# First FFN of a decoder trunk on Trainium2: its input normalized ahead of the products, and a new start for the sum of squares

## Chip, cores and metric

The kernel runs on one core of one Trainium2 chip. The metric is the device time of one execution in microseconds; lower is better. Engines: TensorE (PE: matmuls; PEld: its weight loads), VectorE (DVE), ScalarE (ACT), GpSimd (POOL) and SyncE (SP, which issues the DMA loads).

## The reference

A decoder trunk of two layers on x of 256 tokens by 1024 features, all in float32. Each layer is an FFN half step, a token mixer (retention in layer 0, a short gated convolution in layer 1) and a second FFN half step. Ahead of each of these six sublayers the input is normalized and modulated:

```
def rmsnorm(x, g):
    xf = x.astype(jnp.float32)
    xf = xf * lax.rsqrt(jnp.mean(xf * xf, axis=-1, keepdims=True) + EPS)
    return xf.astype(x.dtype) * g

def modulate(x, g, shift, scale):
    return rmsnorm(x, g) * (1 + scale[:, None, :]) + shift[:, None, :]

def swiglu(h, w_in, w_out):
    gu = h @ w_in
    gate, up = gu[..., :D_FF], gu[..., D_FF:]
    return (jax.nn.silu(gate) * up) @ w_out
```

`shift`, `scale` and `gate` of every sublayer are rows of `silu(c) @ ada_w + ada_b`. A sublayer ends in `x = x + gate * y` (half of it for an FFN). D_FF is 2816, that is 22 tiles of 128. A last rmsnorm gives the output.

## The kernel before

Activations are held transposed: 128 features on the partitions, 256 tokens along the free dimension, so x is eight blocks k of 128x256. To multiply float32 with float32r matmuls, each operand is held as a high half (`hi`, a rounding cast on ScalarE, `split_high`, L248) and the rest (`lo`, a subtraction on VectorE or GpSimd, `split_low`, L253). A product of one 128x128 weight block with one block of h is hi times h's high half, hi times h's low half, and lo times h's high half (`product`, L278). If both halves of h lie side by side in one 512-column tile, the first two are one matmul of 512 columns (L288) whose two half sums are added afterwards; otherwise there are three matmuls of 256 columns (L290 to L292).

Weights stream from memory once, in 1 MB tiles of 128x2048 (`load`, L229), five buffers deep, all issued by SyncE. The weights of the modulation (`ada_w`) come the same way; VectorE multiplies a tile with `cond` (silu of c) and sums it per row in two reductions (`ada_reduce`, L116, its operation at L120). Both kinds of load share the queue.

The first sublayer is an FFN and has a start of its own. `first_modulated` (L464) loads x in four loads, squares it on VectorE and GpSimd, adds the squares in pairs, sums them over the partitions by matmuls with a matrix of ones (`total`, L361: plain f32, two records in the trace for each), and takes the root `std` on ScalarE. `fill` (L428) then issues eight small matmuls whose result nobody reads. For each k it reduces the two `ada_w` halves of that block (shift and scale), scales x by `scale` on ScalarE (L493), adds `std * shift` on VectorE (`halves`, L422, operation at L425), splits the result into halves h, and splits three of four 512-column parts of the weight tile. ScalarE, VectorE and GpSimd run this part in the written order (`manual_schedule`); elsewhere a scheduler orders instructions by priority and dependence.

x is not divided by its root here. h is `x*scale + std*shift`, and since the division is the same for all features of a token, the products are multiplied by r = 1/std afterwards, in `normalized` (L325, operation at L328), one VectorE pass over both halves (gate and up) of a tile as it leaves PSUM.

`first_projections` (L560) multiplies the first eight FFN tiles together, k outermost: in each k block 12 of 16 weight blocks as three matmuls (L579 to L581) and the last four as one plain f32 matmul (L576), into four PSUM tiles. Tiles 8 to 21 follow one at a time through `projections` (L294) with `product`; h's halves lie in a tile 264 wide, so three matmuls are issued. For every tile ScalarE applies silu (L321), VectorE multiplies with the other half (`av`, L592, three buffers), and the result `act` is split (ScalarE cast L334, GpSimd subtraction L335). There are four PSUM tiles of two banks in rotation; after eleven tiles one of them holds `cond` for good (L612).

The later FFNs already work on an h that is normalized whole: `whole` (L434) multiplies x by r (L440), applies scale and shift in one ScalarE `Identity` (L441), and stores both halves side by side in a 512-column slot; `projected` (L307) then issues the 512-column form and adds the half sums with a ScalarE copy (L315) and a VectorE add (L316). Slots come from a pool of 30 shared by `xs`, `whole`, `act` and others.

## Time and profile before

| what | value |
|---|---|
| median of 3 runs | 1078.89 us (1077.05 to 1079.44) |
| the profiled execution's own time | 1079.4 us |
| its span, first to last instruction | 1077.6 us |
| TensorE busy | 1051.5 us (98%), 6642 matmul records |
| VectorE busy | 845.5 us (78%) |
| ScalarE busy | 622.0 us (58%) |
| GpSimd busy | 410.7 us (38%) |
| memory read | 266.20 MB |

Rows of a timeline give the start, the duration, the engine, the line of the kernel, the operation, the tile written and the tiles read, shapes, how many instructions were merged, and in square brackets how long the engine stood idle before and what released it. A matmul's printed duration reaches to its last result, so consecutive matmuls overlap; their pace is read from their starts.

### The profile page before, as it was taken

What the parts mean: (1) busy time and instruction counts of PE and PEld (TensorE: products, weight loads), DVE (VectorE), ACT (ScalarE), POOL (GpSimd) and SP (SyncE); (2) the same over time, 40 slices, a digit from 0 to 9 for tenths busy, and PEclk for the clock granted to TensorE, in tenths of its full rate; (3) what the DMA queues carried; (4) which work ended last, traced back from release to release, by engine and by line L of the source; (5) the groups of instructions that cost most, each with busy time, mean ns of one, the idle gap of its engine ahead of it and who ended that gap; (6) DMA issues with size and microseconds to landing.
All of it is one profiled execution on the core that took longest, in us unless ns stands there. A gap on an engine that the chain in (4) does not pass through costs nothing.

```text
span 1077.6 us, 17508 instructions
## 1 busy us (share of the span) xinstructions
PE 1051.5 (98%) x6642; PEld 945.9 (88%) x6642; DVE 845.5 (78%) x1137; ACT 622.0 (58%) x1048; POOL 410.7 (38%) x357
## 2 busy tenths in 40 slices
PE   8999999999998999999999999999999989999996
PEld 6999988999886889888888988888898889888885
DVE  6899777899658898997777899777799888655444
ACT  4365545763366667566555766655576577655442
POOL 1034356254335432433345243335433433324352
PEclk9999999999999999999999999999999999999999
DMA  9977788868565576787679778777877544554441
GB/s 340 368 277 275 296 279 314 314 224 326 225 234 196 195 290 221 289 325 280 241 234 323 262 294 319 272 253 265 311 254 261 207 161 175 199 201 139 148 134 40
DMA packets 44566, 268.39 MB, mean 249 GB/s; under 512 B 4801, under 2 KB 6977, under 8 KB 19906
## 3 DMA queue, kind: packets, MB, share of 16 engines
q1 hardware_dynamic: 43138, 266.56, 68.1%
q8 instruction: 52, 0.85, 0.3%
q10 hardware_dynamic: 1344, 0.71, 0.2%
q14 instruction: 32, 0.26, 0.1%
HBM read 266.20 MB, written 1.05 MB: 248 GB/s over the span
## 4 chain that ended last, share of the span: by engine, by line
PE 57%; DVE 3%; issue 1%; ACT 0%; DVEq 0%; ACTq 0%
PE ps L288 33%; PE ps L292 19%; PE ps L291 2%; PE ps L290 2%; DVE lo L253 1%; DVE whole L335 0%; DVE rsum L518 0%; PE ps L361 0%; DVE h L415 0%; DVE raw L816 0%; ACT hi L248 0%; DVE xr L440 0%; DVE r L812 0%; DVE sum L328 0%; DVE av L594 0%
## 5 line engine op out<-in xcount | busy, mean ns | idle before, releaser
L253 DVE TENSOR_TENSOR lo<-raw,hi 128x1024 fp32r<-128x1024 f32 (+1 forms) x300 | 370.4, 1244 | 148.9 <-ACT hi L248 138.1
L248 ACT CAST hi<-raw 128x1024 fp32r<-128x1024 f32 (+2 forms) x408 | 377.0, 937 | 167.0 <-PE ps L288 65.5
L288 PE MATMUL ps<-whole,hi 128*128 128x512 f32 x1136 | 398.8, 396 | 2.4 <-ACT std L373 1.6
L292 PE MATMUL ps<-whole,lo 128*128 128x256 f32 x1264 | 353.8, 280 | 0.0
L253 POOL TENSOR_TENSOR lo<-raw,hi 128x384 fp32r<-128x384 f32 (+1 forms) x108 | 202.6, 1877 | 230.0 <-ACT hi L248 228.4
L288 PEld LDWEIGHTS ps<-whole,hi 128*128 128x128 f32 x1136 | 213.7, 188 | 53.3 <-ACT std L373 2.0
L292 PEld LDWEIGHTS ps<-whole,lo 128*128 128x128 f32 x1264 | 239.4, 189 | 0.1
L288 PE MATMUL ps<-act,hi 128*128 128x512 f32 x616 | 217.7, 398 | 0.6 <-DVE rsum L518 0.6
L292 PE MATMUL ps<-act,lo 128*128 128x256 f32 x704 | 197.8, 281 | 0.0
L335 POOL TENSOR_TENSOR act<-av,act 128x256 fp32r<-128x256 f32 x88 | 81.9, 933 | 202.4 <-ACT act L334 201.6
L120 DVE CUSTOM_DVE_ANT_0 raw<-raw,ps,misc 128x1024 f32<-128x1024 f32 x124 | 154.7, 1274 | 0.0
L288 PEld LDWEIGHTS ps<-act,hi 128*128 128x128 f32 x616 | 115.7, 188 | 29.7 <-DVE rsum L518 1.6
L292 PEld LDWEIGHTS ps<-act,lo 128*128 128x128 f32 x704 | 133.1, 189 | 0.3 <-DVE lo L253 0.3
L290 PE MATMUL ps<-h,hi 128*128 128x258 f32 (+1 forms) x464 | 131.8, 284 | 1.0 <-DVE sum L328 0.9
L291 PE MATMUL ps<-h,hi 128*128 128x258 f32 (+1 forms) x464 | 131.0, 282 | 1.5 <-DVE h L415 1.4
L292 PE MATMUL ps<-h,lo 128*128 128x258 f32 (+1 forms) x464 | 130.3, 281 | 0.0
L291 PEld LDWEIGHTS ps<-h,hi 128*128 128x128 f32 x464 | 87.9, 190 | 2.5 <-DVE h L415 2.4
L290 PEld LDWEIGHTS ps<-h,hi 128*128 128x128 f32 x464 | 87.6, 189 | 1.5 <-ACT sg L321 1.1
L292 PEld LDWEIGHTS ps<-h,lo 128*128 128x128 f32 x464 | 87.6, 189 | 0.0
L334 ACT CAST act<-av 128x256 fp32r<-128x256 f32 x88 | 35.3, 405 | 77.0 <-DVE av L592 70.5
L316 DVE TENSOR_TENSOR sum<-ps,sum 128x512 f32<-128x512 f32 x71 | 48.7, 685 | 19.7 <-ACT sum L315 19.7
L321 ACT ACTIVATE sg<-sum 128x256 f32<-128x256 f32 x79 | 32.6, 415 | 47.7 <-DVE sum L316 25.7
(135 smaller groups left out, 1425.4 us busy)
## 6 DMA issues: line engine op xcount, KB each, us to landing
raw<-in_ffn_in SPq DMA_DIRECT2D x80, 1024.0 KB, 4.9
raw<-in_ada_w SPq DMA_DIRECT2D x64, 1024.0 KB, 5.1
raw<-in_ffn_out SPq DMA_DIRECT2D x64, 704.0 KB, 5.1
raw<-in_ada_w SPq DMA_DIRECT2D x16, 512.0 KB, 7.2
raw<-in_ffn_in SPq DMA_DIRECT2D x16, 512.0 KB, 8.2
raw<-in_ret_g SPq DMA_DIRECT2D x8, 1024.0 KB, 4.9
raw<-in_ret_qk SPq DMA_DIRECT2D x8, 1024.0 KB, 5.3
raw<-in_ret_v SPq DMA_DIRECT2D x8, 1024.0 KB, 5.0
```

Of the source, the lines that this page charges most:

```text
L120: ins = nc.vector.tensor_tensor_reduce(out=w, in0=w, in1=state["cond"], scale=1.0, scalar=misc[:, C_ADAB + 72 * l + col:C_ADAB + 72 * l + ...
L248: nc.scalar.copy(out=hi, in_=raw[:, c:c + m])
L253: eng.tensor_tensor(out=lo, in0=raw, in1=hi, op=ALU.subtract)
L288: nc.tensor.matmul(out=ps, lhsT=hi, rhs=m.rearrange("p n s -> p (n s)"), start=start, stop=False)
L290: nc.tensor.matmul(out=ps, lhsT=hi, rhs=m[:, 0], start=start, stop=False)
L291: nc.tensor.matmul(out=ps, lhsT=hi, rhs=m[:, 1], start=False, stop=False)
L292: nc.tensor.matmul(out=ps[:, :n], lhsT=lo, rhs=m[:, 0], start=False, stop=stop)
L316: nc.vector.tensor_tensor(out=y[:, :, :S], in0=ps[:, :, :S], in1=y[:, :, :S], op=ALU.add)
L321: nc.scalar.activation(out=out, in_=y[:, i, :S], func=AF.Silu)
L334: hi = nc.scalar.copy(out=dst[:, 0], in_=src)
L335: lo = eng.tensor_tensor(out=dst[:, 1], in0=src, in1=dst[:, 0].bitcast(F32), op=ALU.subtract)
```

## The change

h of the first FFN is normalized before the products. The reciprocal of `std` is taken at once, after the reductions of block 0; VectorE divides x of block k+1 (`divided`) while block k is split; ScalarE applies scale and shift in one `Identity`, and the halves lie side by side in a slot `whole` of 512 columns. `normalized` is no longer called in this FFN: the first eight tiles go from PSUM to `activate` as they are, and tiles 8 to 21 go through `projected` with its 512-column matmuls, its copy and its add. x comes in two loads of four blocks instead of four of two. The squares of the first half are VectorE's, those of the second half ScalarE's (after `cond`); they are not added in pairs, and `total` takes all eight. GpSimd has no part in the sum, and the Sqrt table is loaded after the squares. The low half of block 0's h is made ahead of its first weight `lo`, that of the others behind it. Instructions that were issued behind the last two of `first_modulated` (one on ScalarE, one on VectorE) are now issued behind one on VectorE.

```
--- before.py
+++ after.py
@@ -98,8 +98,8 @@
             out=ps[:, i, :], lhsT=ones[:1, :], rhs=cond[:1, i * 512:(i + 1) * 512], start=True, stop=True
         )
     conditioned = nc.scalar.activation(out=cond, in_=ps.rearrange("p n c -> p (n c)"), func=AF.Silu)
-    x_pairs = [const.tile([P, 2, S], F32, name=f"x{i}") for i in range(KB // 2)]
-    x = [x_pairs[k // 2][:, k % 2, :] for k in range(KB)]
+    x_quads = [const.tile([P, 4, S], F32, name=f"x{i}") for i in range(KB // 4)]
+    x = [x_quads[k // 4][:, k % 4, :] for k in range(KB)]
 
 
     mod = [const.tile([P, 72], F32, name=f"mod{l}") for l in range(DEPTH)]
@@ -369,8 +369,11 @@
             ps = banks()[:, 0, :S]
         total(parts, ps, start)
         with tc.high_priority(PRIO):
-            std = tmp.tile([P, S], F32, name="std")
-            nc.scalar.activation(out=std, in_=ps, func=AF.Sqrt, bias=eps, scale=1.0 / n_feat)
+            return root(ps, n_feat)
+
+    def root(ps, n_feat):
+        std = tmp.tile([P, S], F32, name="std")
+        nc.scalar.activation(out=std, in_=ps, func=AF.Sqrt, bias=eps, scale=1.0 / n_feat)
         return std
 
     def inverse(std):
@@ -418,12 +421,6 @@
             )
             norm.setdefault("h", []).append(h[:, :, :S1])
             norm["made"] = [hi.ins, lo.ins]
-
-    def halves(l, s, k, xs, std, h):
-
-        shift = mod[l][:, 24 * s + k:24 * s + k + 1]
-        nc.vector.scalar_tensor_tensor(out=xs, in0=std, scalar=shift, in1=xs, op0=ALU.mult, op1=ALU.add)
-        return (h,) + split(h, xs, nc.vector)
 
     def fill(n):
 
@@ -467,45 +464,64 @@
         parts = []
         engines = {mybir.EngineType.Activation, mybir.EngineType.DVE, mybir.EngineType.Pool}
         with tc.manual_schedule(engines=engines):
-            for i, pair in enumerate(x_pairs):
-                nc.sync.dma_start(out=pair, in_=a["x"][:, 2 * i:2 * i + 2, :])
+            for i, quad in enumerate(x_quads):
+                nc.sync.dma_start(out=quad, in_=a["x"][:, 4 * i:4 * i + 4, :])
             nc.scalar.dma_start(out=misc, in_=a["misc"])
             ada = [ada_load(l, s, 0, 2)]
-            with tc.issue_after(conditioned.ins):
-                load_table(AF.Sqrt, ones)
             ps = banks()[:, 0, :S]
-            for i in range(2):
-                sqs = []
-                for j, eng in ((2 * i, nc.vector), (2 * i + 1, nc.gpsimd)):
-                    sq = tmp.tile([P, 2, S], F32, name=f"sq{j}", tag="rot" if i else "sum")
-                    eng.tensor_tensor(out=sq, in0=x_pairs[j], in1=x_pairs[j], op=ALU.mult)
-                    sqs.append(sq)
-                (nc.gpsimd if i else nc.vector).tensor_tensor(out=sqs[0], in0=sqs[0], in1=sqs[1], op=ALU.add)
-                total([sqs[0][:, 0, :], sqs[0][:, 1, :]], ps, i == 0, i == 1)
-            std = tmp.tile([P, S], F32, name="std")
-            nc.scalar.activation(out=std, in_=ps, func=AF.Sqrt, bias=eps, scale=1.0 / D)
+            for i, quad in enumerate(x_quads):
+                for j in range(2):
+                    sq = tmp.tile([P, 2, S], F32, name=f"sq{i}", tag="rot" if i else "sum")
+                    pair = quad[:, 2 * j:2 * j + 2, :]
+                    if i == 0:
+                        nc.vector.tensor_tensor(out=sq, in0=pair, in1=pair, op=ALU.mult)
+                    else:
+                        with tc.issue_after(conditioned.ins):
+                            nc.scalar.activation(out=sq, in_=pair, func=AF.Square)
+                    total([sq[:, 0, :], sq[:, 1, :]], ps, i == 0 and j == 0, i == 1 and j == 1)
+            load_table(AF.Sqrt, ones)
+            std = root(ps, D)
             fill(FILL)
+            ada_reduce(l, s, 0, ada.pop(), True)
+            r = inverse(std)
+
+            def divided(k):
+                if k % 2 == 0:
+                    pairs.append(in_halves(slot(F32, "xs")))
+                xs = pairs[-1][:, k % 2, :]
+                nc.vector.tensor_tensor(out=xs, in0=x[k], in1=r[:, :S], op=ALU.mult)
+                return xs
+
+            pairs = []
+            xs = divided(0)
             for k in range(KB):
-                ada_reduce(l, s, k, ada.pop(), True)
-                if k % 2 == 0:
-                    pair = in_halves(slot(F32, "xs"))
-                xs = pair[:, k % 2, :]
-                nc.scalar.activation(out=xs, in_=x[k], func=AF.Copy, scale=scale_t[l][s][:, k:k + 1])
+                if k:
+                    ada_reduce(l, s, k, ada.pop(), True)
                 raw, width, w = load(2)
                 if k + 1 < KB:
                     ada.append(ada_load(l, s, k + 1, 2))
                 first = split_high(raw, width, w, 512)
-                h = xhl_p.tile([P, 2, HALF], F32R, name=f"h{k}")[:, :, :S]
-                parts.append(halves(l, s, k, xs, std, h))
+                nc.scalar.activation(
+                    out=xs, in_=xs, func=AF.Identity, scale=scale_t[l][s][:, k:k + 1],
+                    bias=mod[l][:, 24 * s + k:24 * s + k + 1],
+                )
+                h = in_halves(slot(F32R, "whole"))
+                nc.scalar.copy(out=h[:, 0], in_=xs)
                 plain.append((xs, raw))
-                split_low(*first, nc.vector)
+                after = divided(k + 1) if k + 1 < KB else None
+                if k:
+                    split_low(*first, nc.vector)
+                made = nc.vector.tensor_tensor(out=h[:, 1], in0=xs, in1=h[:, 0].bitcast(F32), op=ALU.subtract)
+                parts.append(h)
+                if not k:
+                    split_low(*first, nc.vector)
                 for c in range(1, WHOLE // 512):
                     split_low(*split_high(raw, width, w, 512), nc.vector)
                 if k == 1:
                     load_table(AF.Silu, std)
-            r = inverse(std)
-        state["after"] = [i.ins for i in parts[-1][1:]]
-        return [p[0] for p in parts], r
+                xs = after
+        state["after"] = [made.ins]
+        return parts
 
     def residual(n, d, ps):
         l, s = sublayers[n]
@@ -581,7 +597,7 @@
                     nc.tensor.matmul(out=out, lhsT=lo, rhs=h[k][:, 0], start=False, stop=stop)
         return [ps.rearrange("p (n s) -> p n s", s=S) for ps in pss]
 
-    def ffn(n, src=None, h=None, r=None):
+    def ffn(n, src):
         act = []
 
         def activate(y, bias):
@@ -599,15 +615,12 @@
             act.append(t)
 
         if n == 0:
-            for ps in first_projections(h):
-                activate(normalized(ps, r, S), None)
+            for ps in first_projections(src["whole"]):
+                activate(ps, None)
         else:
             src["whole"] = whole(n, src["r"])
         while len(act) < FB:
-            if n:
-                activate(*projected(src))
-            else:
-                activate(normalized(projections(h), r, S), None)
+            activate(*projected(src))
             if n == 0 and len(act) == KEEP:
                 kept = banks().rearrange("p n c -> p (n c)")
                 nc.scalar.copy(out=kept, in_=cond)
@@ -794,7 +807,7 @@
 
     for n, (l, s) in enumerate(sublayers):
         if n == 0:
-            ffn(n, None, *first_modulated())
+            ffn(n, {"whole": first_modulated(), "used": BIASED + 1})
             continue
         h, r, std, begun = modulated()
         src = {"h": h, "r": r, "begun": begun, "used": 0}
```

## Rows read from the trace of the kernel before

**Rows 1.** The page, busy time, share and instructions of each engine.

```profile
PE 1051.5 (98%) x6642; PEld 945.9 (88%) x6642; DVE 845.5 (78%) x1137; ACT 622.0 (58%) x1048; POOL 410.7 (38%) x357
```

**Rows 2.** Table by stage: stretch, length, busy us (instructions) per engine, clock, DMA.

```profile
62.00:80.00 18.00, 17.07 (x144) 16.84 (x143) 17.90 (x22) 11.63 (x22) 9.58 (x8) 1.00 0.65 246
...
100.00:120.00 20.00, 20.00 (x174) 20.00 (x173) 16.61 (x23) 10.50 (x17) 9.28 (x7) 1.00 0.84 331
...
440.00:460.00 20.00, 20.00 (x115) 17.35 (x114) 20.00 (x28) 12.00 (x21) 6.86 (x7) 1.00 0.94 362
...
920.00:940.00 20.00, 20.00 (x117) 17.66 (x116) 12.40 (x15) 11.91 (x21) 7.04 (x6) 1.00 0.61 211
```

**Rows 3.** Timeline of TensorE's matmuls, 0 to 15 us.

```profile
7.47 2.07 PE L361 MATMUL ps<-sq,ones 128*128 128x256 f32 x4 [1.05 <-DVE sq L483]
9.34 1.06 PE L432 MATMUL ps<-cond,ones 128*128 128x128 f32 x4
10.32 1.32 PE L361 MATMUL ps<-sq,ones 128*128 128x256 f32 x4
...
13.86 0.38 PE L579 MATMUL ps<-h,hi 128*128 128x256 f32 x1 [0.88 <-ACT h L334]
```

**Rows 4.** Timeline of VectorE, 5 to 16 us.

```profile
4.77 0.69 DVE L481 TENSOR_TENSOR sq<-x 128x512 f32<-128x512 f32 x1 [4.77 <-DMA x<-in_x]
...
9.64 1.71 DVE L120 CUSTOM_DVE_ANT_0 raw<-raw,cond,misc 128x1024 f32<-128x1024 f32 x1 [1.62 <-DMA raw<-in_ada_w]
...
11.47 1.28 DVE L120 CUSTOM_DVE_ANT_0 raw<-raw,cond,misc 128x1024 f32<-128x1024 f32 x1
...
12.88 0.49 DVE L425 SCALAR_TENSOR_TENSOR xs<-std,mod,xs 128x256 f32<-128x256 f32 x1
```

**Rows 5.** Timeline of ScalarE, 2 to 16 us.

```profile
6.46 1.02 ACT L100 ACTIVATE cond<-ps 128x1024 f32<-128x1024 f32 x1 [2.57 <-PE ps L97]
...
11.74 0.47 ACT L486 ACTIVATE std<-ps,eps 128x256 f32<-128x256 f32 x1 [2.74 <-PE ps L361]
...
13.40 0.40 ACT L334 CAST h<-xs 128x256 fp32r<-128x256 f32 x1 [0.28 <-DVE xs L425]
```

**Rows 6.** Timeline of TensorE, first product of two blocks in a row.

```profile
26.30 0.47 PE L579 MATMUL ps<-h,hi 128*128 128x256 f32 x1
...
32.26 0.47 PE L579 MATMUL ps<-h,hi 128*128 128x256 f32 x1
```

**Rows 7.** Timeline of VectorE, first reduction of two blocks in a row.

```profile
40.04 1.28 DVE L120 CUSTOM_DVE_ANT_0 raw<-raw,cond,misc 128x1024 f32<-128x1024 f32 x1
...
45.95 1.28 DVE L120 CUSTOM_DVE_ANT_0 raw<-raw,cond,misc 128x1024 f32<-128x1024 f32 x1
```

**Rows 8.** Timeline of TensorE, 67 to 70 us.

```profile
67.86 0.28 PE L292 MATMUL ps<-h,lo 128*128 128x256 f32 x1
69.07 0.36 PE L290 MATMUL ps<-h,hi 128*128 128x256 f32 x1 [0.94 <-DVE sum L328]
```

**Rows 9.** Lines L379, L440 and L441: duration in ns, min/median/max.

```profile
L379 DVE RECIPROCAL r<-std x10: 1734/1746/1754, 57.8 to 887.7; 128x256 f32<-128x256 f32 x10
...
L440 DVE TENSOR_TENSOR xr<-x,r x20: 410/416/1115, 217.1 to 896.7; 128x256 f32<-128x256 f32 x20
...
L441 ACT ACTIVATE xr<-xr,mod,sc x40: 586/601/605, 217.8 to 900.2; 128x256 f32<-128x256 f32 x40
```

**Rows 10.** Timeline of GpSimd, 5 to 12 us.

```profile
5.65 1.04 POOL L481 TENSOR_TENSOR sq<-x 128x512 f32<-128x512 f32 x1 [4.68 <-DMA x<-in_x]
7.52 1.39 POOL L481 TENSOR_TENSOR sq<-x 128x512 f32<-128x512 f32 x1 [0.83 <-DMA x<-in_x]
```

**Rows 11.** Timeline of VectorE, 60 to 70 us.

```profile
63.09 2.96 DVE L592 TENSOR_TENSOR av<-sg,sum 128x256 f32<-128x256 f32 x2
```

**Rows 12.** Timeline of TensorE, at 348 us.

```profile
347.70 0.70 PE L361 MATMUL ps<-acc,ones 128*128 128x256 f32 x2 [3.36 <-POOL acc L351]
```

**Rows 13.** Table by stage, as above, at 350 us.

```profile
350.00:352.00 2.00, 2.00 (x7) 1.71 (x7) 2.00 (x3) 0.38 (x1) 0.00 (x0) 0.50 0.00 0
```

## Prediction

> **What bounds the kernel now.** I read the page first. TensorE is busy for 98% of the span [rows 1], so time comes back only where it waits or where a product gets cheaper. Its busy time is partly modelled, so I then read the table by stage. It is full in the stage of one tile after another and in later sublayers [rows 2]. The exception in this FFN is 62 to 80 us: 17.07 of 18 us, with VectorE at 17.90 of 18. The timelines then give three places where the change can act.
>
> First, the start. The first product of the network begins at 13.86 [rows 3]. Ahead of it VectorE does two reductions over the ada weights (9.64 and 11.47) and the multiply-add with `std` (12.88) [rows 4], and ScalarE the root at 11.74 and the cast of h at 13.40 [rows 5]. Second, the first stage (the eight k blocks of `first_projections`): TensorE starts a block at 26.30 and the next at 32.26, 5.96 us, back to back [rows 6]; VectorE's round is 45.95 - 40.04 = 5.91 [rows 7]. Both are nearly tight, TensorE a little more. Third, the hand-over to the tile stage: TensorE stands 0.94 us before 69.07 because VectorE's `normalized` has not freed a PSUM tile [rows 8].
>
> **The change part by part.** The change adds no TensorE column anywhere except in the sum of squares. From 13.86 to 142 us TensorE has next to no slack, so I cost (a) when the first product starts, (b) the block period, (c) the wait at 69 us, (d) the price of a product, and (e) what lies behind.
>
> (a) Start. Removed: the multiply-add with `std` and ScalarE's `Copy`. Added in the chain ahead of the first product: the reciprocal 1.75, the division of x 0.42, and an `Identity` with scale and shift, 0.60 [rows 9]; the cast stays at 0.40. Counted from the moment t0 when VectorE has both `std` and the end of its two reductions (its order is by hand, reductions first), the first product comes at t0 + 1.75 + 0.42 + 0.60 + 0.40 + about 0.2 for the handovers = t0 + 3.4. Before, it was 12.88 to 13.86 = 1.0.
>
> When is t0? The reductions: the first took 1.71, the second 1.28, for the same shape [rows 4]; GpSimd was squaring and adding during the first [rows 10]. GpSimd now has no such work, so the pair ends some 0.4 earlier, near 12.35, if the weights land no earlier than at 9.6. The Trainium skill (SBUF — State Buffer, section "Who interferes with whom") says that a VectorE instruction with two SBUF inputs contends with a GpSimd one that reads SBUF. By that rule the 0.43 is GpSimd's doing; without it the pair would end at 12.75 and t0 be the same, since `std` is later.
>
> `std`: two of four x tiles had landed by 5.65, the last by 7.52 [rows 10]; the two larger loads carry the same bytes in the same order, so I take the same moments. VectorE squares the first half (0.69 each, [rows 4]), so these are ready at 6.3 and 7.0. TensorE is free at 6.4, when ScalarE's `cond` starts on its first matmuls [rows 5]. ScalarE squares the second half after `cond` (from 7.5); the nearest row, `cond` itself, takes 1.02 for twice the columns [rows 5], so one square lies between 0.5 and 1.0; at 0.6 they are ready at 8.1 and 8.7, at 1.0 at 8.5 and 9.5, and don't bind. TensorE binds: the sums of pairs are gone, so it takes eight f32 matmuls where it took four, 16 records for 8. Four records took 9.34 - 7.47 = 1.87, or 0.47 each, early, and 1.32, or 0.33 each, from 10.32 on [rows 3]. The clock column prints 1.00 there, but the early spacing is that of the lower of the two levels (1.2 GHz). All sixteen slow would end at 6.4 + 7.5 = 13.9, all fast at 11.7. I take 12.2, near the fast end, because the rise had come by 11 us before and TensorE is now busier ahead of it. With the root (0.47, [rows 5]) and a handover, t0 = 12.8 and the first product is at 16.2: **+2.3 us**. The ends are 15.7 (+1.8) and 17.9 (+4.0).
>
> (b) Blocks. VectorE loses 0.49 [rows 4] and gains 0.42 [rows 9] per block, and its 0.47 wait for the cast is filled by the next division and a `lo`: 5.91 falls to about 5.3. The new chain from the reductions to h is `Identity` and cast, 0.60 + 0.40, about as long as the old 0.49 + 0.40. TensorE needs 5.96 whatever VectorE does [rows 6]. The cover for the extra 0.1 is the 0.6 us by which VectorE now gains on TensorE in each round. **0 us**; without that cover at most 0.1 in each of seven blocks.
>
> (c) Hand-over. The reciprocal and eight `normalized` (0.69 each) leave VectorE just where it was full (0.69 is what a VectorE pass over 128x512 takes, [rows 4]), 7 us in all, and it reaches the end of the first stage earlier. PSUM is now released by `av`, behind ScalarE's `silu`, but the first tiles are complete some microseconds before TensorE returns to their banks. What is late next is `av` with its three buffers, which GpSimd frees; two of them took 2.96 us at 63 us, where one operation of that shape takes 0.42 [rows 9, 11]. Gain **-1.1 us** (67.86 to 69.07 less the 0.12 of a matmul); the ends are 0 and -1.3. By the rule of the skill named above an `av` that reads PSUM has one SBUF input and stands clear of GpSimd, which speaks for the gain; no row here shows such an `av`.
>
> (d) Tiles 8 to 21: 224 products, each three matmuls of 256 columns before, now one of 512 and one of 256. In 20 us TensorE issues 174 records as triples, 58.0 products; as pairs 115 in one stage and 117 in another, 57.5 and 58.5 [rows 2]. A product costs 0.345 us either way, give or take 3 ns: 224 x 3 ns = 0.7 us to either side. I take **0**. VectorE's 0.69 for `normalized` becomes an add of that size; ScalarE gets a copy of 128x512, at the same estimate of 0.6 some 8 us over the 14 tiles, where it is half idle (10.50 of 20 us, [rows 2]).
>
> (e) Behind it: slots. Eight whole h, and 22 act, fill the 30 slots once the four `xs` slots are free, which they are after the first stage. The later sublayers run the same code on the same data. 0.
>
> Sum: +2.3 - 1.1 = **+1.2 us** on the profiled execution's own 1079.4 (span 1077.6 and 1.8 around it), 1080.6. That execution lies 0.5 above the median of 1078.89, from which the sum gives 1080.1. I forecast 1080.3: no change that can be told, since this kernel's own runs spread by 2.4 us and about 0.2%, 2.2 us, is what a measurement tells from no change.
>
> **Rivals.** *Slower, by the clock at the start* (0.17). The one mechanism is that TensorE stays at its lower level through the sixteen records and into the first products. For it: four early records at 0.47 each; the wait from the last fill to the first product grows from 0.88 [rows 3] to over 2 us; and later in this trace a wait of 3.36 us [rows 12] was followed by a granted clock of 0.50, 7 matmuls in 2 us [rows 13] where 11.5 are usual [rows 2]. Against: a 2 us wait is shorter, and the level had risen by 11 us before. Price: the start at +4.0, and about 3.4 us of products at half speed, +1.7; less 1.1: 1084.0. It decides once the root ends after 13.5.
>
> *The wait at 69 us stays* (0.13), because `silu` and `av` release PSUM later than `normalized` did. For it: the slow `av` [rows 11]. Against: VectorE's lost work. +2.3: 1081.7.
>
> *Everything at its better end* (0.15): start +1.8, wait -1.3, pairs -0.7: 1079.2, no change again. Only a further saving, such as the half-clock stretch at 348 us not recurring (-1.7), would make it faster: 1077.5 and less.
>
> *Weight loads bound the triples* (0.03). TensorE's loads are busy 20.00 of 20.00 us with triples and 17.35 with pairs [rows 2]. If they set the pace, dropping one load in three would cut each tile's 5.6 us to 3.7: -26 us, 1054. Against: pairs with idle loads issue no more products per 20 us than triples. The Trainium skill (Perfetto Trace Analysis, section "Identifying the Most-Contended Engine") wants TensorE judged by the busy share of its weight loads; by that rule this rival would be the forecast, and the rows with pairs disagree.
>
> **How the numbers follow.** The forecast's case has 0.52 (its own range 1078.6 to 1082.0). Of it 0.05 falls above +0.2% (1081.05). The clock rival is slower throughout; of the lasting wait half is. Slower: 0.05 + 0.17 + 0.06 = 0.28. Faster: the weight loads and 0.06 of the better ends, 0.09. The same: 0.63. The range reaches down to 1077.5 (better ends with the later half-clock gone) and up to 1083.3, short of the full clock rival, leaving 0.1 out on each side.
>
> **What would show it.** The first product near 16.2 and the reciprocal at 12.8; blocks still 5.96 apart with VectorE idle in each round; no VectorE wait at the ninth and tenth tile; the 512-column matmul 0.23 us ahead of its 256-column partner. The prediction fails if the first product starts before 15 or after 17.5, if blocks get longer or shorter, or if 20 us of the tile stage hold more than 59 products.

## Result and the profile after

| what | before | after |
|---|---|---|
| median of 15 runs each | 1079.25 us (1076.87 to 1082.25) | 1082.42 us (1080.10 to 1083.84) |
| ratio after to before | | 1.0025, interval 1.0014 to 1.0035 |
| profiled execution's own time, and its span | 1079.4, 1077.6 | 1080.39, 1078.6 |
| first product | 13.86 | 17.53 |
| second block begins | 20.33 | 25.55 |
| tile 8 begins | 62.14 | 67.81 |
| output products begin | 142.37 | 145.66 |
| next sublayer begins | 205.56 | 207.95 |

The change makes the kernel slower by 0.25%, between 1.5 and 3.8 us of 1079; the two medians lie 3.17 us apart. The range (1077.5 to 1083.3) holds the new time. The likeliest case, no change that can be told, is missed narrowly: the difference is clear of zero and lies above the prediction's own line of 0.2%, though the interval reaches below that line. The second likeliest, slower, is what came. The rows from "first product" on are starts of TensorE's first matmul of that part, from its timeline. Read downwards, the difference between the two columns is +3.67, +5.22, +5.67, +3.29 and +2.39 us: a loss at the start, a second one in block 0, a small one over the blocks, and two gains behind them. After 207.95 the same code runs on the same data, and there the profiled execution of after happened to take 1.4 us less (870.6 from the next sublayer to the end of the span, for 872.0); the last section shows that this differs from one execution to the next.

The page's line on busy time, which answers to [rows 1], shows 216 records fewer and TensorE still at 98%:

```profile
PE 1052.7 (98%) x6426; PEld 940.9 (87%) x6426; DVE 834.2 (77%) x1128; ACT 630.7 (58%) x1064; POOL 409.2 (38%) x354
```

The table by stage of after, with the columns of [rows 2]: first the start, then the stretches shown for before.

```profile
15.00:18.00 3.00, 0.40 (x2) 0.20 (x2) 2.20 (x5) 1.53 (x4) 0.00 (x0) 1.00 1.02 412
18.00:20.00 2.00, 2.00 (x10) 1.82 (x11) 2.00 (x4) 1.04 (x2) 0.00 (x0) 0.69 1.04 414
20.00:22.00 2.00, 2.00 (x11) 2.00 (x11) 1.97 (x4) 0.00 (x0) 0.00 (x0) 0.50 0.93 373
22.00:24.00 2.00, 2.00 (x18) 2.00 (x17) 1.73 (x6) 1.59 (x4) 0.00 (x0) 0.96 0.46 154
...
62.00:80.00 18.00, 18.00 (x114) 16.29 (x113) 12.86 (x16) 14.13 (x27) 12.15 (x9) 1.00 0.82 321
100.00:120.00 20.00, 20.00 (x117) 17.48 (x116) 16.83 (x24) 12.77 (x20) 9.01 (x6) 1.00 0.86 348
```

From 15 to 18 us TensorE stands; from 18 to 24 us the granted clock is 0.69, 0.50 and 0.96, so for some 3.4 us it is at the lower of its two levels (1.2 GHz), in the middle of block 0's products: 11 of them in 2 us where 18 fit once the level is back. Between 62 and 80 us TensorE is full and VectorE has fallen from 17.90 of 18 to 12.86.

TensorE's timeline of before, the start of its second block:

```profile
20.33 0.47 PE L579 MATMUL ps<-h,hi 128*128 128x256 f32 x1
```

TensorE's timeline of after: the start, the first product of two blocks, the change to the tile stage.

```profile
6.61 3.78 PE L361 MATMUL ps<-sq,ones 128*128 128x256 f32 x8 [0.22 <-DVE sq L477]
10.18 1.49 PE L429 MATMUL ps<-cond,ones 128*128 128x128 f32 x6
11.46 2.13 PE L361 MATMUL ps<-sq,ones 128*128 128x256 f32 x8
13.43 1.28 PE L429 MATMUL ps<-cond,ones 128*128 128x128 f32 x10
17.53 0.39 PE L595 MATMUL ps<-whole,hi 128*128 128x256 f32 x1 [2.83 <-ACT whole L509]
...
25.55 0.47 PE L595 MATMUL ps<-whole,hi 128*128 128x256 f32 x1
...
31.59 0.47 PE L595 MATMUL ps<-whole,hi 128*128 128x256 f32 x1
...
66.70 1.46 PE L592 MATMUL ps<-xs,raw 128*128 128x256 f32 x6
67.81 0.58 PE L288 MATMUL ps<-whole,hi 128*128 128x512 f32 x1
68.23 0.28 PE L292 MATMUL ps<-whole,lo 128*128 128x256 f32 x1
68.35 0.40 PE L288 MATMUL ps<-whole,hi 128*128 128x512 f32 x1
```

The sum of squares is two groups of eight records (L361) with six records of `fill` (L429) between them, which takes 11.46 - 10.18 = 1.28 us: TensorE has no written order, and the scheduler put part of the filling between the two halves of the sum, whose second squares were ready by 9.12 (ScalarE's row at 7.97, below). The first group goes at about 0.45 us a record, the second at about 0.25, as the level rises near 12. Then `fill` ends and TensorE waits 2.83 us for `whole` (0.88 for h before, [rows 3]). Block 0 runs from 17.53 to 25.55, 8.02 us, for 6.47 before; the next takes 6.04, for 5.96 [rows 6]. There is no wait at 67.81, nor one behind it up to the next sublayer.

VectorE and ScalarE of after, their timelines.

```profile
9.41 1.28 DVE L120 CUSTOM_DVE_ANT_0 raw<-raw,cond,misc 128x1024 f32<-128x1024 f32 x1 [2.26 <-DMA raw<-in_ada_w]
...
10.81 1.28 DVE L120 CUSTOM_DVE_ANT_0 raw<-raw,cond,misc 128x1024 f32<-128x1024 f32 x1
...
14.19 1.75 DVE L382 RECIPROCAL r<-std 128x256 f32<-128x256 f32 x1 [2.10 <-ACT std L376]
```

```profile
7.97 1.15 ACT L480 ACTIVATE sq<-x 128x512 f32<-128x512 f32 x2 [0.53 <-DMA x<-in_x]
...
13.69 0.47 ACT L376 ACTIVATE std<-ps,eps 128x256 f32<-128x256 f32 x1 [3.05 <-PE ps L361]
...
16.44 0.60 ACT L504 ACTIVATE xs<-xs,mod,sc 128x256 f32<-128x256 f32 x1 [1.77 <-DVE xs L492]
17.07 0.40 ACT L509 CAST whole<-xs 128x256 fp32r<-128x256 f32 x1
```

The reductions are done at 12.10; VectorE then waits 2.10 us for `std`. The reciprocal starts at 14.19, and the first product 3.34 us later.

### The profile page after: what moved, and what is told of

The parts are those of the page before. It is cut to its first block, busy times and chain, and to the rows that moved or that the text cites. A ratio compares the mean times of both kernels' runs of the same rounds, so it can differ in the third digit from the quotient of the medians.

```text
span 1078.6 us, 17044 instructions
## 1 busy us (share of the span) xinstructions
PE 1052.7 (98%) x6426; PEld 940.9 (87%) x6426; DVE 834.2 (77%) x1128; ACT 630.7 (58%) x1064; POOL 409.2 (38%) x354
## 4 chain that ended last, share of the span: by engine, by line
PE 57%; DVE 3%; issue 0%; ACT 0%; DVEq 0%; ACTq 0%
PE ps L288 33%; PE ps L292 19%; PE ps L291 2%; PE ps L290 2%; DVE lo L253 1%; DVE h L418 0%; DVE whole L335 0%; PE ps L361 0%; DVE rsum L534 0%; DVE raw L829 0%; ACT hi L248 0%; DVE xr L437 0%; DVE r L825 0%; DVE sum L328 0%; DVE av L610 0%
## 5 line engine op out<-in xcount | busy, mean ns | idle before, releaser
L288 PE MATMUL ps<-whole,hi 128*128 128x512 f32 x1360 | 474.4, 394 | 2.4 <-ACT std L376 1.6
L292 PE MATMUL ps<-whole,lo 128*128 128x256 f32 x1488 | 416.9, 280 | 0.0
L288 PEld LDWEIGHTS ps<-whole,hi 128*128 128x128 f32 x1360 | 255.4, 188 | 60.2 <-ACT std L376 2.0
L292 PEld LDWEIGHTS ps<-whole,lo 128*128 128x128 f32 x1488 | 282.4, 190 | 0.1
L316 DVE TENSOR_TENSOR sum<-ps,sum 128x512 f32<-128x512 f32 x85 | 58.1, 684 | 21.9 <-ACT sum L315 21.9
L291 PE MATMUL ps<-h,hi 128*128 128x258 f32 x240 | 68.9, 287 | 2.2 <-DVE h L418 2.1
L290 PE MATMUL ps<-h,hi 128*128 128x258 f32 x240 | 68.9, 287 | 0.0
L292 PE MATMUL ps<-h,lo 128*128 128x258 f32 x240 | 68.1, 284 | 0.0
L315 ACT COPY sum<-ps 128x512 f32<-128x512 f32 x85 | 49.0, 576 | 1.5 <-PE ps L292 1.5
L344 ACT ACTIVATE sq<-x 128x256 f32<-128x256 f32 x48 | 19.8, 417 | 51.0 <-DVE x L537 43.5
L291 PEld LDWEIGHTS ps<-h,hi 128*128 128x128 f32 x240 | 45.7, 190 | 3.4 <-DVE h L418 3.0
```

The source lines that it names most:

```text
L288: nc.tensor.matmul(out=ps, lhsT=hi, rhs=m.rearrange("p n s -> p (n s)"), start=start, stop=False)
L290: nc.tensor.matmul(out=ps, lhsT=hi, rhs=m[:, 0], start=start, stop=False)
L291: nc.tensor.matmul(out=ps, lhsT=hi, rhs=m[:, 1], start=False, stop=False)
L292: nc.tensor.matmul(out=ps[:, :n], lhsT=lo, rhs=m[:, 0], start=False, stop=stop)
L315: nc.scalar.copy(out=y[:, :, :S], in_=ps[:, :, S:])
L316: nc.vector.tensor_tensor(out=y[:, :, :S], in0=ps[:, :, :S], in1=y[:, :, :S], op=ALU.add)
```

## Experiments

Times of a stage are read from one profiled execution of each kernel. Each run's product time is the length of the tile stage (start of tile 8 to the first output product) over its 224 products: 0.347 us in after, 0.353 in before once the 1.1 us of its wait [rows 8] are taken off. Some 0.5 us of the latter is still lost time: by the starts in TensorE's timeline, before is also 0.3 us late at 80.9 and 0.1 at 97.8, and its undisturbed tiles take 5.60 us, 0.350 a product.

**The start, four kernels** (before: median 1080.21).

`fill_behind` holds the filling back until the sum is done:

```
-            nc.tensor.matmul(
+            last = nc.tensor.matmul(
...
+        return last
...
-            fill(FILL)
+            with tc.issue_after(summed.ins):
+                fill(FILL)
```

> The changed kernel with the eight fill matmuls queued behind the last matmul of the sum of squares (three of them stood in its middle). Theory S (the loss is the start: sixteen plain f32 records at the lower clock and three fills between them hold up the root, and the long wait before the first product costs the clock): the six fill records took 1.28 us in the middle, so the root starts near 12.4 instead of 13.69 and the first product near 16.2 instead of 17.53; with a wait of 2.3 us instead of 2.8 the fall of the clock may stay, and block 0 takes 6.5 us without it or 8.0 with it. Total 1.3 us less, or 2.9 with the clock held. Theory R (the loss lies behind the start, in blocks of 6.04 instead of 5.96 us and in how the products run): the first product moves, the total does not.

`fill_long` is the same with `FILL = 18` for 8, so that it reaches as far as the first product.

> The same with 18 fill matmuls instead of eight, so that TensorE is busy until shortly before the first product. Theory S: 36 records of 0.11 us reach from 12.2 to about 16.1, the clock stays at its full level, the first product comes near 16.2 and block 0 takes 6.5 us instead of 8.0; tile 8 starts near 64.9 instead of 67.81 and the total falls by 2.9 us, to about the time of the kernel before or a little below. Theory R: block 0 is still 8 us long, since something else holds it, or the total does not follow.

`sum_as_before` is after with the old sum: four loads of x, squares on VectorE and GpSimd, the adds in pairs, four f32 matmuls, the Sqrt table early.

> The changed kernel with the start of the kernel before: x in four loads, squares on VectorE and GpSimd, added in pairs, four matmuls, Sqrt table early. Theory S: root near 11.74, VectorE free of its reductions at 12.75, first product near 16.1 (12.75 and 3.4), 1.4 us earlier than in the changed kernel; the fills end near 13.0, so the wait is 3.1 us and the clock falls as it does there (block 0 of 8.0 us). Total 1.4 us less. If the f32 records and the fills were not what held the root, the first product stays near 17.5.

`before_new_sum` is before with the new sum alone: two loads, squares on VectorE and ScalarE, eight f32 matmuls.

> The kernel before with only the new start: x in two loads, squares on VectorE and ScalarE, eight matmuls, Sqrt table late. Nothing is divided early. Theory S: the root ends at 14.16 as in the changed kernel, the multiply-add and the cast follow, first product near 15.2 instead of 13.86; the wait is 0.7 us, the clock holds, block 0 takes 6.5 us. Total 1.3 us more than the kernel before, so the other half of the changed kernel's delay is the reciprocal and the clock. Theory R: less than 0.5 us, since VectorE's round of 5.91 and TensorE's of 5.96 take some of it back.

| kernel | root (`std`) begins | first product | block 0 | tile 8 | next sublayer | median | ratio to before |
|---|---|---|---|---|---|---|---|
| before | 11.74 | 13.86 | 6.47 | 62.14 | 205.56 | | |
| after | 13.69 | 17.53 | 8.02 | 67.81 | 207.95 | 1082.42 | 1.0025 (1.0014 to 1.0035) |
| fill_behind | 11.64 | 15.49 | 7.86 | 65.61 | 205.75 | 1081.28 | 1.0011 (0.9999 to 1.0023) |
| fill_long | 12.18 | 16.03 | 6.54 | 64.83 | 204.97 | 1078.57 | 0.9991 (0.9978 to 1.0004) |
| sum_as_before | 13.14 | 16.98 | 7.46 | 66.72 | 206.86 | 1082.29 | 1.0016 (1.0008 to 1.0025) |
| before_new_sum | 12.52 | 14.40 | 6.47 | 62.68 | 205.77 | 1079.92 | 1.0000 (0.9990 to 1.0009) |

The two kernels with the filling behind the sum differ in its length alone. The table by stage, first of `fill_behind`, then of `fill_long`, and of each the row of TensorE's timeline for the first product:

```profile
16.00:18.00 2.00, 2.00 (x10) 1.93 (x11) 2.00 (x4) 1.10 (x2) 0.00 (x0) 0.55 1.03 414
18.00:20.00 2.00, 2.00 (x12) 2.00 (x12) 1.97 (x4) 0.00 (x0) 0.00 (x0) 0.60 1.02 406
```

```profile
15.49 0.39 PE L597 MATMUL ps<-whole,hi 128*128 128x256 f32 x1 [2.16 <-ACT whole L511]
```

```profile
16.00:18.00 2.00, 1.93 (x12) 1.51 (x12) 1.99 (x4) 1.65 (x3) 0.00 (x0) 1.00 1.05 420
18.00:20.00 2.00, 2.00 (x19) 2.00 (x18) 1.97 (x5) 0.00 (x0) 0.00 (x0) 1.00 1.00 399
```

```profile
11.92 4.18 PE L430 MATMUL ps<-cond,ones 128*128 128x128 f32 x36
16.03 0.39 PE L597 MATMUL ps<-whole,hi 128*128 128x256 f32 x1
```

`fill_long` did what it was expected to do. With 36 records of filling up to the first product (no wait before 16.03) the clock column stays at 1.00 and block 0 takes 6.54 us; with 16 and a wait of 2.16 it falls to 0.55 and block 0 takes 7.86. So the fall of the clock costs 1.3 to 1.5 us, and the wait ahead of the first product brings it. In `fill_behind` itself the expectation had left open whether it would fall. In before, a wait of 0.88 did not bring it, nor did one of 0.86 in `before_new_sum`.

The first product follows the reciprocal's start by 3.34 us in after and in both of these kernels, so what varies at the start is the root. Taking the six records of filling out of the sum brought it forward by 2.05 us here: 1.28 of that is their own time, 0.25 an earlier start of the sum (6.36 for 6.61), and the rest goes with the clock, which had risen at 9.36 in this execution and at 11.93 in the one of after. `sum_as_before` missed its expectation of a root near 11.74: with the old sum, half the records, the root came at 13.14. The sum began 0.65 us later there than in before (8.12 for 7.47), and its second half took 1.87 us for some 1.3, since the level rose only at 13.3. `before_new_sum` missed the 1.3 us that were expected of it too: the level rose at 9.63, and the doubled sum cost 0.54 us of the first product and nothing that the medians tell. The new sum by itself is thus a small loss where the level rises early; at the lower level each of its records takes 0.45 us. These are single executions, and the moment of the rise is scattered in them.

`after_again` is the kernel after, once more, to see how firm its profile is.

> The changed kernel once more. Theory S holds the start for a matter of when the clock rises: 11.93 in the first trace, 9.4 to 13.3 in the others; the first product of another execution moves with it, by at most 1.5 us from 17.53, and the clock falls again behind the long wait. The stage from tile 8 to the first output matmul is again 77.8 to 77.9 us, unless the pace of pairs changes from one execution to the next (0.347 or 0.353 us, 1.5 us on this stage).

One run, 1083.68: first product 18.13, block 0 8.01, tile stage 77.85, next sublayer 208.54, with the level rising at 12.93. The picture of after repeats, 0.6 us later. In `three_matmuls`, `three_padded` and `passes_back` below, whose start is that of after, the level rose at 11.57, 11.10 and 11.05 and the first product came at 17.48, 17.02 and 16.96. So one and the same start moves by 1.2 us from execution to execution, and in all five the clock fell behind a wait of 2.83 us.

**The blocks and the tile stage, four kernels.** `three_matmuls` has tiles 8 to 21 multiplied with three matmuls from the same `whole`, without copy and add:

```
-            activate(*projected(src))
+            activate(*(projected(src) if n else (projections(src["whole"]), None)))
```

> The changed kernel with tiles 8 to 21 as three matmuls of 256 columns on the same normalized h, without copy and add. Read in the stage from tile 8 to the first output matmul, 77.85 us in the changed kernel and in fill_behind, fill_long and sum_as_before. Theory C (a product costs its columns, as the prediction had it, within 3 ns): 224 products at 0.350 us, 78.4 to 78.6 us. Theory P (the pace of a triple depends on where the two halves of h lie: the blocks on side-by-side halves take 6.04 us in every kernel that has them and 5.96 in the two on the 264-wide tile, and triples on side-by-side halves in later sublayers go at 0.360): 224 x 0.360, 80.8 us.

`three_padded` also puts h back into its own tiles, halves 264 apart instead of 256:

```
-                h = in_halves(slot(F32R, "whole"))
+                h = xhl_p.tile([P, 2, HALF], F32R, name=f"h{k}")[:, :, :S]
```

> The same three matmuls, with the halves of h in the 264-wide tile of the kernel before (1056 bytes apart instead of 1024), normalized as in the changed kernel. Theory P: blocks back at 5.96 us, the stage from tile 8 at 78.5. Theory C or another cause of the longer blocks (VectorE's and ScalarE's new order): blocks stay at 6.04.

`passes_back` gives VectorE its nine operations of 7 us back at the hand-over (a reciprocal nobody reads, and `normalized` of the first eight tiles by a tile of ones):

```
+            inverse(std)
...
+            one = tmp.tile([P, HALF], F32, name="r")
+            nc.gpsimd.memset(one, 1.0)
...
-                activate(ps, None)
+                activate(normalized(ps, one, S), None)
```

> The changed kernel with VectorE's old work put back where it was, as work without effect: a reciprocal after the eight blocks, and a pass that multiplies the first eight tiles with ones as they leave PSUM. Theory H1 (that work made the wait at the ninth tile): TensorE waits about 1 us there again and the stage from tile 8 takes 78.9 us. Theory H2 (VectorE's lead covers it: its last lo of block 7 ends 7.7 us before tile 8 starts, 4.3 in the kernel before, because its round is shorter): no wait, 77.9 us.

`padded_h` is `fill_long` with h in tiles 264 wide and the 512-column form on them:

```
-                h = in_halves(slot(F32R, "whole"))
+                h = xhl_p.tile([P, 2, HALF], F32R, name=f"h{k}")[:, :, :S]
...
+                    out=ps.rearrange("p (n s) -> p n s", n=2), lhsT=hi, rhs=m, start=start, stop=False
```

> fill_long with the halves of h in the 264-wide tile; the 512-column matmul then reads two runs of 256 columns. Theory P: blocks of 5.96 us instead of 6.04, tile 8 starts 0.6 us earlier relative to the first product than in fill_long (48.8 us), and if pairs keep 0.347 us the first output matmul comes near 142.1; median 0.6 us below fill_long's. Theory C: as fill_long. If a moving operand in two runs is slower, the stage from tile 8 grows beyond 77.85.

| kernel | h's halves | form in tiles 8 to 21 | a block | tile stage | a product |
|---|---|---|---|---|---|
| before | 264 apart | three matmuls | 5.96 | 80.23, 1.1 of it a wait | 0.353 (0.350 undisturbed) |
| three_padded | 264 apart | three matmuls | 5.97 | 78.62 | 0.351 |
| three_matmuls | 256 apart | three matmuls | 6.04 | 80.82 | 0.361 |
| padded_h | 264 apart | pairs | 5.97 | 78.59 | 0.351 |
| after | 256 apart | pairs | 6.04 | 77.85 | 0.347 |
| passes_back | 256 apart | pairs | 6.04 | 81.45, 1.65 of it a wait | 0.354 behind the wait |

`three_matmuls` and `three_padded` have one run each, 1085.03 and 1082.04 us; `padded_h` has a median of 1079.28, 0.9988 of before's 1081.20 (0.9977 to 0.9998), which cannot be told from `fill_long`. The table by stage, 100 to 120 us, of `three_matmuls`, `three_padded` and `padded_h`, one fence each:

```profile
100.00:120.00 20.00, 20.00 (x169) 20.00 (x169) 13.92 (x18) 9.19 (x14) 7.57 (x6) 1.00 0.88 344
```

```profile
100.00:120.00 20.00, 20.00 (x174) 20.00 (x174) 13.68 (x18) 9.60 (x14) 5.88 (x6) 1.00 0.96 373
```

```profile
100.00:120.00 20.00, 20.00 (x116) 17.55 (x116) 15.96 (x22) 11.48 (x19) 8.26 (x7) 1.00 0.86 348
```

169 records as triples from the new tiles, 174 from the padded ones: 56.3 and 58.0 products in 20 us, with VectorE far from full in both. The new home of h makes triples dearer by 3%. The blocks of the first stage are made of such triples, and their period follows the same line: 6.04 with the new tiles, 5.97 with the padded ones, whatever the tile stage does. Pairs escape this, 0.347 in the new tiles here (0.354 in other executions, see below), and in `padded_h`, where the 512-column matmul reads two runs, they take 0.351: the expectation's last branch, a stage longer than 77.85. What these runs show is that the tile decides; that it is the distance of the halves (1024 bytes, for 1056) and not their place in memory was not separated.

`passes_back` (one run, 1086.37) shows no wait where before had it. Its table by stage at the hand-over, tile 8 beginning at 67.18, answers to before's row from 62 to 80 [rows 2]:

```profile
67.00:85.00 18.00, 18.00 (x102) 15.39 (x101) 17.89 (x22) 11.79 (x24) 10.32 (x10) 1.00 0.70 244
```

TensorE's timeline, and VectorE's ahead of the wait that it has:

```profile
90.06 0.28 PE L292 MATMUL ps<-whole,lo 128*128 128x256 f32 x1
92.00 0.51 PE L288 MATMUL ps<-whole,hi 128*128 128x512 f32 x1 [1.65 <-DVE sum L316]
```

```profile
86.24 3.41 DVE L120 CUSTOM_DVE_ANT_0 raw<-raw,cond,misc 128x1024 f32<-128x1024 f32 x1
...
91.26 1.28 DVE L316 TENSOR_TENSOR sum<-ps,sum 128x512 f32<-128x512 f32 x2
```

With the 7 us back, VectorE is full (19.52 of the 20 us from 80 on), and TensorE waits 1.65 us for its `sum`, 23 us after the place it waited in before. The reduction of 3.41 us (1.28 alone, above) ran beside two GpSimd operations of 2.57 and 1.72 us, at 86.00 and 88.53. After has one as long, 3.42, at 84.3, and no wait: only where VectorE has no slack does it cost anything. So neither theory held whole. At the hand-over H2 was right: VectorE is as full as in before (17.89 of 18 us for 17.90), and TensorE is full all the same. VectorE comes to this work with a longer lead there: its last `lo` of block 7 ends 8.1 us ahead of tile 8, in before 4.3 (7.9 in `fill_long`, so the slow block 0 is not the reason). Further on the lead is used up, and a wait is back, larger and later than H1 had placed it. So the lead suffices to take away the wait at the ninth tile; being rid of the passes is what keeps TensorE from waiting later. What makes the lead was not tested by itself.

**Putting the better parts together, three kernels** (before: median 1080.72 for the first two, 1080.43 for the third). `pairs_and_fill` is after with a sum that avoids the low clock's price: x in four loads, three of four squares on VectorE and one on ScalarE, pairs added on VectorE, four f32 matmuls, the filling behind the sum with `FILL = 16`.

> The changed kernel with a start made from the earlier runs: x in four loads again, three squares on VectorE and one on ScalarE, added in pairs on VectorE, so four f32 matmuls instead of eight, and 16 fill matmuls queued behind them. Theory S: the sum ends near 10.6, the root near 11.1, VectorE's reductions (12.2) bind instead, first product near 15.6 (2 us before the changed kernel), the clock holds and block 0 takes 6.5 us; first output matmul near 142.2 as in the kernel before, next sublayer 1 us before that kernel's 205.56, since the stages from tile 8 on keep their 3.3 us. Median 1 us below the kernel before and 4 below the changed one. If the clock still falls, 1.5 us of it is lost.

`early_warm` adds four matmuls ahead of everything else on TensorE:

```
+    early = banks()[:, 1, :P]
+    for _ in range(4):
+        warm = nc.tensor.matmul(out=early, lhsT=ones, rhs=ones, start=True, stop=True)
```

> pairs_and_fill with four matmuls of ones ahead of everything on TensorE, from about 1 us. If TensorE's level follows what it did before, it rises earlier than the 9.4 to 13.3 us of the runs so far and the sum takes 0.25 us per record instead of 0.43; but the first product stays near 15.6, because the reductions bind, and the median equals pairs_and_fill within 0.5 us. If the level does not follow so little work, nothing changes at all. Against both: if the sum still binds, the first product comes up to 1 us earlier than in pairs_and_fill.

`first_tiles_first` is `pairs_and_fill` with the first eight tiles' activations ahead of weight casts:

```
-                activate(ps, None)
+                with tc.high_priority(PRIO):
+                    activate(ps, None)
```

> pairs_and_fill with the silu, av and split of the first eight tiles given priority over the splitting of later weights. Theory V (pairs_and_fill's wait of 1.13 us at tile 8 is the rival of the prediction in another place: PSUM is now released by silu and av, and ScalarE had two weight casts, 1.99 us, ahead of the second silu): the two silus come first, tile 8 starts at 64.2 without a wait, the first output matmul at 142.1 if pairs go at 0.347 us and at 143.6 at 0.353, next sublayer between 204.3 and 205.8; median 1 us or more below pairs_and_fill relative to the kernel before. If the wait was for the weights of tile 8, it stays or grows, since their casts come later.

| kernel | first product | block 0 | tile 8 | tile stage | next sublayer | median | ratio to before |
|---|---|---|---|---|---|---|---|
| pairs_and_fill | 15.31 | 6.53 | 65.34 | 79.24 | 207.08 | 1081.27 | 1.0006 (0.9993 to 1.0019) |
| early_warm | 15.46 | 6.53 | 65.48 | 79.25 | 207.22 | 1081.26 | 1.0012 (1.0000 to 1.0024) |
| first_tiles_first | 15.46 | 6.54 | 64.27 | 77.85 | 204.41 | 1077.37 | 0.9972 (0.9963 to 0.9981) |

`pairs_and_fill` missed its expectation. The start came as hoped, and block 0 kept the clock, but TensorE then waited at the hand-over. TensorE's and ScalarE's timelines of `pairs_and_fill`, and the latter's of `first_tiles_first`:

```profile
65.34 0.50 PE L288 MATMUL ps<-whole,hi 128*128 128x512 f32 x1 [0.87 <-DVE av L612]
```

```profile
61.20 0.41 ACT L334 CAST act<-av 128x256 fp32r<-128x256 f32 x1 [0.49 <-DVE av L612]
61.51 1.99 ACT L248 CAST hi<-raw 128x1024 fp32r<-128x1024 f32 x2
63.41 0.65 ACT L321 ACTIVATE sg<-ps 128x256 f32<-128x256 f32 x2
```

```profile
60.48 0.38 ACT L321 ACTIVATE sg<-ps 128x256 f32<-128x256 f32 x1 [4.96 <-PE ps L601]
61.36 0.38 ACT L321 ACTIVATE sg<-ps 128x256 f32<-128x256 f32 x1 [0.49 <-DVE av L612]
61.64 0.40 ACT L334 CAST act<-av 128x256 fp32r<-128x256 f32 x1
61.93 1.05 ACT L248 CAST hi<-raw 128x1024 fp32r<-128x1024 f32 x1
```

In `pairs_and_fill` ScalarE takes two weight casts (1.99 us, 61.51) before the second tile's silu at 63.41; `av` of that tile is late, and so is its PSUM tile. In `first_tiles_first` the second silu is at 61.36, TensorE begins tile 8 at 64.27 without a wait, and no wait of TensorE is left up to the next sublayer, which begins 1.15 us earlier than in before. This is the mechanism of the prediction's second rival (PSUM released by `silu` and `av`); after itself escaped it, with a second silu at 65.21, ahead of such casts. The wait is not the whole of the difference between the two profiled executions: of 2.67 us at the next sublayer, 1.07 are there at tile 8, and 1.39 come from pairs that go at 0.354 in `pairs_and_fill` and 0.347 in `first_tiles_first`, without a wait and without a cause found. `early_warm` moved nothing: its level rose at 12.36, its first product is at 15.46, and the wait at the hand-over stayed.

`first_tiles_first` is 0.28% under before, about as far under it as after is over it, and the intervals lie far apart; it met its expectation.

## Why the prediction was right and where it was wrong

**(a) Start: the chain right, t0 wrong.** From t0 to the first product the prediction had 3.4 us; it is 3.34. Against before that chain costs +2.4, of the +3.67 measured. The rest is t0, put at 12.8 and found at 14.19. Three items were in it. The reductions behaved as costed: 1.28 each without GpSimd beside them, done at 12.10, earlier than the 12.35 written (the rule quoted there from the Trainium skill, SBUF — State Buffer, "Who interferes with whom", agrees with this pair). ScalarE's squares took 0.6 each and did not bind. The sum did: it was to end at 12.2, "near the fast end, because the rise had come by 11 us before and TensorE is now busier ahead of it". It ended 1.4 us later, at about 13.6. 1.28 us of that are the fill records in its middle, which before has too (four, at 9.34 in [rows 3]) and which the estimate left out; 0.2 are its later start (6.61 for 6.4). The sixteen records themselves took about 5.5 us, no more than the 5.8 allowed, though the level rose at 11.93, no earlier for the busier engine: half of them went slow, half fast. The first product at 17.53 is just over the line of 17.5 that the prediction had named for its own failure, and inside its upper end of 17.9; with this start's scatter (16.96 to 18.13) it could have come out on either side of that line.

**The clock rival: right in its second half.** The level did not stay low through the sixteen records; it rose at 11.93 and fell again at 18.76, in the first products. The rival was to decide once the root ends after 13.5; the root ended at 14.16. After a wait of 2.83 us the granted clock was 0.50 for some 3.4 us, as long as the rival had it, and block 0 grew by 1.55 where the rival had 1.7. "A 2 us wait is shorter" was the argument against it, and it did not hold: `fill_behind` lost the clock after 2.16. The rival's total, 1084.0, came out lower because the tile and output stages gave back more than its 1.1. This rival deserved more than 0.17.

**(b) Blocks: 0 us predicted, +0.45 found.** VectorE's round did not bind, as said: it is idle in the rounds. But the triples became dearer, and `three_matmuls`, `three_padded` and `padded_h` give the cause: the tile in which h lies. The prediction took the block's 5.96 as TensorE's need "whatever VectorE does", and forgot that its operand moves. "If blocks get longer" was its second sign of failing, and they did.

**(c) Hand-over: -1.1 predicted, about -1.6 found.** No wait of TensorE at the ninth or tenth tile; VectorE went from 17.90 to 12.86 of 18 us. The changed kernel with the old tiles and the old form, `three_padded`, has a tile stage of 78.62 us for 80.23, so 1.6 us were lost in before: the wait, and 0.4 us of small delays at 80.9 and 97.8. The prediction gave two reasons, that VectorE is rid of 7 us and that it "reaches the end of the first stage earlier". `passes_back` separates them: the second is enough at the ninth tile, and without the first a wait comes at 92. In `pairs_and_fill` another took its place just ahead of tile 8, at 65.3, that of ScalarE's order. The slow `av` that spoke for the second rival did not recur in the first eight tiles: all eight, which read PSUM in after, took 0.41 to 0.42 us, where the second in before, reading `sum`, took 2.62.

**(d) Products: 0 give or take 0.7 predicted, -0.8 found.** 77.85 us in after for 78.62 in `three_padded`, 0.347 a product for 0.351. That is the edge of the forecast, and luck has a part in it: the pairs of `pairs_and_fill`, same form and same tiles, ran at 0.354 and took 79.24, 0.6 us more than padded triples. The gain of pairs is real only against triples from the new tiles (0.361). The rival by which weight loads bound the triples is refuted: they are busy 20.00 of 20.00 us with 56.3 products and with 58.0, and 17.5 with 58. The Trainium skill's Perfetto Trace Analysis, "Identifying the Most-Contended Engine", judges TensorE's headroom by MFU (the share of its peak rate) and by the busy share of its weight loads; by the loads alone pairs would have had room that triples lack, and these runs disagree with that.

**(e) Behind it: 0 predicted, -0.9 found.** The output stage takes 62.29 for 63.19. In before TensorE waited 0.57 us in it for VectorE's `rsum`, and the matmuls around this place cost the other 0.3; in after it does not wait. TensorE's timeline of before:

```profile
156.55 0.50 PE L288 MATMUL ps<-act,hi 128*128 128x512 f32 x1 [0.57 <-DVE rsum L518]
```

The cause is open. `passes_back`, with VectorE's passes put back, has no wait there either (62.50), so being rid of them does not explain it. VectorE ran three weight `lo` in a row ahead of that `rsum` in before (5.14 us from 150.96) and one in after (1.23 us at 157.27); what put them so was not tested.

Summed up to the next sublayer: +3.67, +1.55, +0.45, -2.38 (c and d) and -0.90 make +2.39, for the +1.2 predicted. The step that failed is (a): the moment of t0, with the fill records inside the sum put at nothing, and the clock that is lost behind the long wait. That the new time still lies inside the range is luck in part: of the 3.28 us gained behind the blocks the prediction had 1.1, and without the other 2.2 the loss would have been near the full clock rival.

## What to carry to other kernels

When work moves ahead of the first product, price the wait that it opens on TensorE, and fill it: here 20 more fill records cost nothing and saved 1.3 to 1.5 us of half-clock products, and filling that a scheduler may put between the parts of a sum must be held behind it. When an operand moves to another tile, its layout is part of the change; measure the same matmuls from both. And when a buffer's release passes from one engine to another, see what the new releaser has queued ahead of it, since one priority on the first eight tiles is all that differs between the medians 1081.3 and 1077.4.

## What the runs showed of the hardware

- The level of TensorE's clock rose at quite different moments of the start, between 9.4 and 13.3 us, in kernels with like work ahead (9.36 in `fill_behind`, 9.63 in `before_new_sum`, 10.14 in `fill_long`, 11.93 in after, 12.36 in `early_warm`, 12.93 in `after_again`, 13.3 in `sum_as_before`); four matmuls more from 0.99 us on, in `early_warm`, did not bring it forward (12.45 in `pairs_and_fill`, without them). The remaining traces have it between 10.7 and 12.2. While it is low, a plain f32 record of 256 columns takes 0.45 us.
- Triples of 256-column matmuls take 0.361 us from halves that lie side by side in a 512-column tile and 0.351 from the padded tiles; pairs take 0.347 or 0.354 and 0.351.
- Pairs from a 512-column tile run at one of two paces, also in code that no change touches and in two executions of one kernel. The table by stage at 490 us, in the second FFN, of before, after and `after_again`:

```profile
490.00:510.00 20.00, 20.00 (x115) 17.33 (x115) 17.27 (x20) 11.95 (x21) 5.71 (x5) 1.00 0.83 304
```

```profile
490.00:510.00 20.00, 20.00 (x118) 17.64 (x116) 16.12 (x19) 12.40 (x20) 7.47 (x7) 1.00 0.87 315
```

```profile
490.00:510.00 20.00, 20.00 (x115) 17.36 (x114) 15.53 (x20) 12.40 (x21) 8.19 (x8) 1.00 0.82 308
```

115 or 118 records of the same pairs in 20 us, at a granted clock of 1.00 in all three. That FFN's products from `whole` take 108.56, 106.60 and 108.55 us (429.66 to 538.22, 432.29 to 538.89, 433.47 to 542.02): two levels 2 us apart, and each of the other eleven profiled executions shows one of the two, within 0.1 us. That is more than most terms of this study's sums and about half the spread of one kernel's runs. It outweighs the 1.4 us that the profiled execution of after gained behind 207.95. The first FFN's 0.347 and 0.354 are the same two paces: 16 products take 5.55 us throughout its tile stage in `first_tiles_first` and 5.66 in `pairs_and_fill`, and in the second FFN 5.55 in after and 5.66 in `after_again`. What sets the pace was not found.
